# Low parts of 256-column weights placed 192 bytes, not 64, into their buffers

## The chip, the cores and the metric

The kernel runs on one core of a Trainium2 chip. The metric is the device time of one execution in microseconds (us). Before the change it is 1455.13 us, the median of three runs (1454.99 to 1455.19).

## What is computed

A decoder trunk of two layers works on one sequence of 512 tokens with a model width of 1024, all in 32-bit floats. Cut to what matters here:

```
h = rmsnorm(x, g_mix)
z = h @ w_in                      # q, k, v, retention q, k, v, g, two gates
ya = window_attention(...) @ w_a
yb = retention(...) @ w_b
mixed = sigmoid(ga) * ya + sigmoid(gb) * yb
x = x + mixed @ w_out
h2 = rmsnorm(x, g_mlp)
x = x + square(relu(h2 @ w_up)) @ w_down
```

At the end stands one more rmsnorm. Nearly all the arithmetic is in the products with the weight matrices.

## The kernel before, in words

**High and low parts.** TensorE multiplies numbers of a shortened 32-bit type. To keep the precision, every operand is split into a high part (the number rounded to that type) and a low part (the rest, rounded again), and a product of two operands is made of three matmuls: high x high, high x low, low x high. The function `products` (lines 389 to 397) issues the three; line 395 multiplies the first operand's high part with the second's high part, line 396 the first's high part with the second's low part, line 397 the first's low part with the second's high part. In a matmul the first operand is the weights, loaded into TensorE's array by an instruction of its own (PEld in the profile), and the second operand is moved through it column by column. So lines 395 and 396 load the same high part of the weights, and line 397 loads the low part. In the profile's rows the moving operand is named first: `mm<-xl,hi` moves xl past the weights hi.

**Weight units.** The weight matrices come in units of 128 x 1024 numbers. The order of the units is written out in `unit_order`. `load_until` issues their transfers into the buffers `raw`, a few units ahead (AHEAD = 4), and `split_until` (from line 322) makes the parts: ScalarE writes `hi` (line 343), VectorE subtracts and writes `lo` (line 344). `hi` and `lo` have four buffers each (SPLIT + 1). `unit` hands the two parts to the stage that multiplies with them.

**Seven products instead of eight.** The up projection, the down projection, the values of the retention and the output projection (w_out) are made with a block scheme that replaces eight products of half-size blocks by seven products of sums of blocks. The sums of weight blocks are made partly by transfers that add (GpSimd's queue), partly on VectorE. Two of these stages have moving operands of 256 columns, with the weight parts `hi` and `lo` as the weights: the units named "pair" (w_up; the function `pair`, through `products`, lines 395 to 397) and the units named "wo" (w_out; the function `output`, line 1301, which issues hi, hi, lo for each place). In all other stages 512 columns are moved, or `hi` and `lo` are the moving operand.

**Where the parts lie.** A line here is LINE = 16 numbers, 64 bytes in each of the 128 partitions. Each buffer of `hi` and `lo` has UNIT + 4 * LINE = 1088 numbers, 4352 bytes, so that the part can be placed some lines into it:

```
LINE = 16
ASIDE = ("pair", "wo")
...
            aside = LINE if name in ASIDE else 0
            hi, lo = (
                wpool.tile([P, UNIT + 4 * LINE], F32R, tag=n, name=n, bufs=SPLIT + 1)[:, aside : aside + UNIT]
                for n in ("hi", "lo")
            )
```

In the units "pair" and "wo" both parts begin 64 bytes into their buffers, in all others at the buffer's start. In the memory that the program is given, the buffers of `hi` and `lo` and those of the moving operands (`xh`, `xl`, `r0` to `r7`, `late`) all begin 128 bytes past a multiple of 256, and each matmul's columns begin a multiple of 512 bytes further on. So the weights of a matmul lie 64 bytes from its moving rows, modulo 256, in "pair" and "wo", and 0 bytes from them in the rest. This distance is what the text calls the distance.

**The order of the work.** The order on each engine is set when the program is built. In a "pair" stage each of 28 pairs makes 7 x 12 = 84 matmuls of 256 columns (2352), and between two pairs' groups stand the 512-column matmuls of the down projection. "wo" has 7 x 48 = 336 matmuls in each layer (672).

Of the kernel before, what the change touches and what calls it, by code (L numbers as in the profile page):

```python
# [11 lines left out]
F32R = mybir.dt.float32r  # L12
# [5 lines left out]
P = 128  # L18
# [27 lines left out]
N_PAIR = 14  # L46
UNIT = 1024
LINE = 16
ASIDE = ("pair", "wo")
WARM = 8  # L50
PACE = 0.8
DEEP = 3
# [2 lines left out]
SPLIT = 3  # L55
# [62 lines left out]
def decoder(ctx, tc, xT, x_first, w_in, w_rv, w_a, w_b, w_wo, w_up, w_pair, w_down, w_end, tables, decay, band, g_last, out):  # L118
# [4 lines left out]
    wpool = ctx.enter_context(tc.tile_pool(name="wpool", bufs=3))  # L123
# [6 lines left out]
    def f32(ap):  # L130
        return ap.bitcast(F32)
# [36 lines left out]
    def halves(i):  # L168

        return (slice(0, UNIT // 2), slice(UNIT // 2, UNIT)) if i < 3 else (slice(0, UNIT),)  # L170
# [11 lines left out]
    def load_until(n):  # L182
        while state["loaded"] < min(n, len(order)):
            i = state["loaded"]
            layer, name, j = order[i][:3]
            if name == "pair":
                load_part(i)
            elif name == "block":
                load_block(i)
            elif name in MIXING:  # L190
                load_values(i)
            else:
                raws[i] = raw_tile()
                for at in halves(i):
                    queue = nc.scalar if i == 0 and at.start == 0 else nc.sync
                    source = w_end[j] if name == "w_end" else weights[name][layer, j]
                    queue.dma_start(raws[i][:, at], source[:, at])
                    if i < 3:
                        load_x()
            state["loaded"] += 1  # L200
# [77 lines left out]
    def add_part(i):  # L278
        if order[i][3] in (1, 2):
            last = raws.pop(i - 1)  # L280
            at = LEFT if order[i][3] == 1 else RIGHT
            nc.vector.tensor_tensor(raws[i][:, at], last[:, LEFT], last[:, RIGHT], ALU.add)
# [18 lines left out]
    def add_block(i):  # L301
        e, part = order[i][2:]
        if part in (2, 4) and e < N_BLOCK - 1:
            raws[i] = raws.pop(i - 2)
            nc.vector.tensor_tensor(raws[i], raws[i], raws.pop(i - 1), ALU.add)
# [10 lines left out]
    def add_values(i):  # L316
        part = order[i][2]
        if part in (2, 4):
            raws[i] = raws.pop(i - 2)
            nc.vector.tensor_tensor(raws[i], raws[i], raws.pop(i - 4), ALU.add)  # L320

    def split_until(n):
        while state["split"] < min(n, len(order)):
            i = state["split"]
            name, part = order[i][1], order[i][-1]
            if name in MIXING:
                add_values(i)
            load_until(i + AHEAD)
            if name == "pair":
                add_part(i)  # L330
            elif name == "block":
                add_block(i)
            raw = raws[i]
            aside = LINE if name in ASIDE else 0
            hi, lo = (
                wpool.tile([P, UNIT + 4 * LINE], F32R, tag=n, name=n, bufs=SPLIT + 1)[:, aside : aside + UNIT]
                for n in ("hi", "lo")
            )
            for at in (LEFT,) if name == "pair" and part == 3 else halves(i):
                if i == 0 and at.start == 0:  # L340
                    nc.vector.tensor_copy(hi[:, at], raw[:, at])
                else:
                    state["high"] = nc.scalar.activation(hi[:, at], raw[:, at], AF.Copy).ins  # L343
                nc.vector.tensor_tensor(lo[:, at], raw[:, at], f32(hi[:, at]), ALU.subtract)  # L344
            kept = {
                "pair": part < 2,
                "block": name == "block" and part < 4 and order[i][2] < N_BLOCK - 1,
                **{n: name == n and order[i][2] < 4 for n in MIXING},
            }
            if not kept.get(name):  # L350
                raws.pop(i)
            parts[i] = (hi, lo)
            state["split"] += 1

    def unit(name, layer):
        i = state["next"]
        assert order[i][:2] == (layer, name), (order[i], layer, name)
        state["next"] += 1
        hold = state["hold"]
        split_until(i + SPLIT + 1 if hold is None else max(i + 1, min(hold, i + SPLIT + 1)))  # L360
        return parts.pop(i)
# [257 lines left out]
    def layer_body(layer):  # L619
# [1006 lines left out]
        class Ending:  # L1626
# [74 lines left out]
            def first_weights(self):  # L1701
                with tc.issue_after(self.turned):
                    split_until(state["next"] + 1)
# [67 lines left out]

    scaled_input(0, 0)
    split_until(1)
    for u in (2, 3):
        for k in (2 * u - 3, 2 * u - 2):
# [170 lines left out]
```

## Time and profile before

| | |
|---|---|
| median of three runs | 1455.13 us |
| the profiled execution, its own time | 1457.31 us |
| its span, first to last instruction | 1455.2 us |
| mean granted clock of TensorE | 0.999 |
| instructions in the span | 22150 |
| busiest part of the chain that ended last | TensorE (matmuls of the product lines) |

The profile is of one execution. Its page gives the busy time of each engine (PE is TensorE's matmuls, PEld its weight loads, DVE VectorE, ACT ScalarE, POOL GpSimd, SP the engine that issues most transfers), the chain of work that ended last, and the costliest groups of instructions. A row of a group has the line, the engine, the operation, the tiles written and read, the shape, the count, the busy time in us, the mean length of one in ns, and the idle time of the engine before it with what ended that. Matmuls overlap in their pipeline: the length of one in a row is not its share of the time. How fast they follow each other is read from the starts, in the timeline (start in us, length in us, engine, line, tiles, shape, count) or in the chain of waits, where neighbours of one line are merged (start, length, line, count).

### The profile page before, as it was taken

The numbers are of one execution on the slowest core, as the hardware profiler recorded it, in microseconds if no ns is written. First come the engines' busy times: TensorE is split into PE (matmuls) and PEld (weight loads), VectorE is DVE, ScalarE is ACT, GpSimd is POOL, SyncE is SP. The second block draws the span as 40 slices with busy tenths as digits, with TensorE's granted clock in tenths as the row PEclk, the third lists the DMA queues.
The fourth block names the chain that finished last, engine by engine and source line by source line (L and its number), as shares of the span: only waits on it lengthen the run. The fifth ranks groups of instructions, "written<-read, shape, count | busy, mean of one in ns | idle before, by whom it ended". The sixth has DMA issues, their size and how long they took to land.

```text
span 1455.2 us, 22150 instructions
## 1 busy us (share of the span) xinstructions
PE 1443.0 (99%) x8041; PEld 1258.8 (87%) x8041; DVE 1167.0 (80%) x1762; ACT 969.2 (67%) x1592; POOL 222.6 (15%) x329
## 2 busy tenths in 40 slices
PE   9999999999999999999999999999999999999998
PEld 7888888888988999999888888888889799999997
DVE  6978876866998888888778788687778988787885
ACT  6657555543687777777756575565437877777775
POOL 0011012112101111112201110112120011111120
PEclk9999999999999999999999999999999999999999
DMA  7598359799745677666955983797875477777664
GB/s 258 177 290 225 105 165 303 237 247 248 232 124 196 191 200 186 175 182 179 310 177 170 295 222 108 215 293 223 221 214 175 138 202 199 195 193 197 177 188 149
DMA packets 96428, 297.57 MB, mean 204 GB/s; under 512 B 11328, under 2 KB 11456, under 8 KB 90432
## 3 DMA queue, kind: packets, MB, share of 16 engines
q0 software_dynamic: 35936, 125.58, 37.2%
q1 hardware_dynamic: 59664, 169.27, 33.5%
q8 instruction: 63, 1.03, 0.3%
q10 hardware_dynamic: 720, 1.31, 0.2%
q14 instruction: 45, 0.37, 0.1%
HBM read 256.54 MB, written 115.87 MB: 256 GB/s over the span
## 4 chain that ended last, share of the span: by engine, by line
PE 94%; DMA 2%; ACT 2%; DVE 1%; issue 1%; SPq 0%; DVEq 0%; ACTq 0%
PE mm L395 23%; PE mm L396 23%; PE mm L397 22%; PE wo L1301 5%; PE b L395 2%; PE b L396 2%; PE b L397 2%; PE rv L396 2%; PE rv L395 2%; PE rv L397 2%; PE mm L410 2%; DMA raw<-w_pair_in 1%; PE score L778 1%; PE pT L743 1%; PE r L397 1%; PE r L396 1%
## 5 line engine op out<-in xcount | busy, mean ns | idle before, releaser
L343 ACT ACTIVATE hi<-raw 128x1024 fp32r<-128x1024 f32 (+1 forms) x387 | 394.3, 1021 | 257.5 <-PE mm L396 137.1
L344 DVE TENSOR_TENSOR lo<-raw,hi 128x1024 fp32r<-128x1024 f32 (+1 forms) x388 | 452.3, 1173 | 105.8 <-ACT hi L343 104.4
L395 PE MATMUL mm<-xh,hi 128*128 128x512 f32 (+1 forms) x976 | 343.1, 355 | 1.6 <-ACT xh L418 0.9
L396 PE MATMUL mm<-xl,hi 128*128 128x512 f32 (+1 forms) x976 | 343.6, 355 | 0.0
L397 PE MATMUL mm<-xh,lo 128*128 128x512 f32 (+1 forms) x976 | 339.5, 354 | 0.0
L395 PEld LDWEIGHTS mm<-xh,hi 128*128 128x128 f32 x976 | 183.9, 189 | 27.6 <-ACT xh L418 1.6
L396 PEld LDWEIGHTS mm<-xl,hi 128*128 128x128 f32 x976 | 185.0, 190 | 24.2
L397 PEld LDWEIGHTS mm<-xh,lo 128*128 128x128 f32 x976 | 182.7, 188 | 23.6
L397 PE MATMUL mm<-r,lo 128*128 128x256 f32 (+1 forms) x608 | 187.9, 309 | 0.0
L396 PE MATMUL mm<-r,hi 128*128 128x256 f32 (+1 forms) x608 | 187.9, 309 | 0.0
L395 PE MATMUL mm<-r,hi 128*128 128x256 f32 (+1 forms) x608 | 185.6, 309 | 0.5 <-ACT mm L1476 0.5
L395 PEld LDWEIGHTS mm<-r,hi 128*128 128x128 f32 x608 | 114.7, 189 | 8.5 <-ACT mm L1476 0.7
L396 PEld LDWEIGHTS mm<-r,hi 128*128 128x128 f32 x608 | 115.2, 189 | 7.8
L397 PEld LDWEIGHTS mm<-r,lo 128*128 128x128 f32 x608 | 114.1, 188 | 6.2
L1624 POOL DMA_DIRECT2D y<-eu x56 | 62.3, 1351 | 370.8 <-DVE eu L1609 370.2
L396 PE MATMUL mm<-lo,r 128*128 128x512 f32 (+1 forms) x276 | 104.6, 388 | 0.0
L397 PE MATMUL mm<-hi,r 128*128 128x512 f32 (+1 forms) x276 | 101.3, 387 | 0.0
L395 PE MATMUL mm<-hi,r 128*128 128x512 f32 (+1 forms) x276 | 98.4, 390 | 0.9 <-ACT eu L1619 0.6
L395 PE MATMUL b<-hi,r 128*128 128x512 f32 x180 | 70.5, 392 | 1.6 <-DVE eu L1609 1.2
L396 PE MATMUL b<-lo,r 128*128 128x512 f32 x180 | 70.3, 390 | 0.0
L1301 PE MATMUL wo<-r,hi 128*128 128x256 f32 x384 | 68.0, 281 | 0.0
L397 PE MATMUL b<-hi,r 128*128 128x512 f32 x180 | 67.9, 390 | 0.0
(323 smaller groups left out, 2679.5 us busy)
## 6 DMA issues: line engine op xcount, KB each, us to landing
raw<-w_in_in SPq DMA_DIRECT2D x73, 512.0 KB, 5.9
sums_down<-w_down_in POOLq DMA_DIRECT2D x30, 1024.0 KB, 11.6
sums_up<-w_pair_in POOLq DMA_DIRECT2D x56, 512.0 KB, 10.5
raw<-w_down_in SPq DMA_DIRECT2D x45, 512.0 KB, 7.8
raw<-w_pair_in SPq DMA_DIRECT2D x84, 256.0 KB, 3.7
y<-y POOLq DMA_DIRECT2D x63, 256.0 KB, 9.2
y<-eu POOLq DMA_DIRECT2D x61, 256.0 KB, 8.0
raw<-sums_down SPq DMA_DIRECT2D x30, 512.0 KB, 7.3
```

What stands on the lines that cost most here:

```text
L343: state["high"] = nc.scalar.activation(hi[:, at], raw[:, at], AF.Copy).ins
L344: nc.vector.tensor_tensor(lo[:, at], raw[:, at], f32(hi[:, at]), ALU.subtract)
L395: nc.tensor.matmul(ps, ah, bh, start=start and i == 0, stop=False, **more)
L396: nc.tensor.matmul(ps, ah, bl, start=False, stop=False, **more)
L397: latest[0] = nc.tensor.matmul(ps, al, bh, start=False, stop=stop and i == n - 1, **more).ins
L410: latest[0] = nc.tensor.matmul(ps, w[:, cols(j, c)], moving[k][low], start=first, stop=bool(final)).ins
L743: nc.tensor.transpose(pt[:, i * P : (i + 1) * P], sm[:, at : at + P], ident)
L778: nc.tensor.matmul(ps[:, g * w : (g + 1) * w], q_s[g][:, c, at], part[:, keys], start=i == 0, stop=i == 1)
L1301: latest[0] = nc.tensor.matmul(o, w[:, cols], v, start=start and first and n % 2 == 0 and w is hi and v is vh, stop=final and w is lo, ski ...
L1624: nc.gpsimd.dma_start(y[:, 2 * j + m, i * T : (i + 1) * T], t, **how)
```

## The change

In the units "pair" and "wo" the low part begins 3 * LINE = 48 numbers, 192 bytes, into its buffer. The high part stays at 64 bytes. All other units stay at 0. No buffer moves and no size changes; the instructions that carry another address are the 140 subtractions of line 344 that write these low parts and the 1008 matmuls that have them as weights.

```diff
-ASIDE = ("pair", "wo")
+NARROW = ("pair", "wo")
+ASIDE = (LINE, 3 * LINE)
...
             raw = raws[i]
-            aside = LINE if name in ASIDE else 0
             hi, lo = (
-                wpool.tile([P, UNIT + 4 * LINE], F32R, tag=n, name=n, bufs=SPLIT + 1)[:, aside : aside + UNIT]
-                for n in ("hi", "lo")
+                wpool.tile([P, UNIT + 4 * LINE], F32R, tag=n, name=n, bufs=SPLIT + 1)[:, at : at + UNIT]
+                for n, at in zip(("hi", "lo"), ASIDE if name in NARROW else (0, 0))
             )
```

The distance between the low part and the moving rows becomes 192 bytes modulo 256 in these units, that of the high part stays 64.

## The prediction

> **What bounds the kernel now.** I read the page first: which engine is busy, and what the chain that ended last is made of.
>
> ```profile
> PE 1443.0 (99%) x8041; PEld 1258.8 (87%) x8041; DVE 1167.0 (80%) x1762; ACT 969.2 (67%) x1592; POOL 222.6 (15%) x329
> PE 94%; DMA 2%; ACT 2%; DVE 1%; issue 1%; SPq 0%; DVEq 0%; ACTq 0%
> ```
>
> Of the span of 1455.2 us TensorE is idle for 12.2 us, and 94% of the chain is its own work. So the time is the sum of the steps from one matmul's start to the next one's start. What a change does to a step, it does to the end. The change touches matmuls of 256 moving columns only, so the next view is the groups of TensorE by line and shape.
>
> ```profile
> L395 PE MATMUL mm<-r,hi 128*128 128x256 f32 x448 | 125.8, 281 | 0.5 <-ACT mm L1476 0.5
> L397 PE MATMUL mm<-r,lo 128*128 128x256 f32 x448 | 125.7, 280 | 0.0
> L395 PE MATMUL mm<-xh,hi 128*128 128x256 f32 x336 | 94.1, 282 | 0.1
> L397 PE MATMUL mm<-xh,lo 128*128 128x256 f32 x336 | 92.1, 281 | 0.0
> L1301 PE MATMUL wo<-r,hi 128*128 128x256 f32 x384 | 68.0, 281 | 0.0
> L1301 PE MATMUL wo<-r,lo 128*128 128x256 f32 x192 | 53.7, 281 | 0.0
> L1301 PE MATMUL wo<-late,hi 128*128 128x256 f32 x64 | 11.6, 281 | 0.2 <-ACT xh L418 0.2
> L1301 PE MATMUL wo<-late,lo 128*128 128x256 f32 x32 | 8.9, 279 | 0.0
> ```
>
> Lines 395 and 396 hold the same weights, so line 396 has the counts of line 395. That makes 3 x (448 + 336) = 2352 matmuls in the "pair" units and 672 in the "wo" units, 3024 in all. A third of them, 448 + 336 + 192 + 32 = 1008, use a low part as weights. The 281 ns in these rows is the time from a matmul's start to its end; matmuls overlap, so this number says nothing of the step. The step is read from the starts. In the chain of waits the "wo" matmuls stand merged (start, length, count):
>
> ```profile
> 365.69 32.13 PE wo L1301 x273
> 399.78 5.70 PE wo L1301 x48
> ...
> 1086.05 33.92 PE wo L1301 x288
> 1120.85 5.46 PE wo L1301 x48
> ```
>
> 33.92 / 288 = 117.8 ns and 32.13 / 273 = 117.7 ns a step, but 5.46 / 48 = 113.8 ns in the last product of layer 1, with the same shape and the same placement of the weights. (The 48 of layer 0 begin with a wait, so their mean is higher.) The timeline shows the same two speeds in the "pair" units (the rows between are left out, with their count below):
>
> ```profile
> 466.15 0.63 PE L395 MATMUL mm<-hi,r 128*128 128x512 f32 x2
> ...
> 466.74 0.28 PE L396 MATMUL mm<-r,hi 128*128 128x256 f32 x1
> ...
> 467.87 0.28 PE L397 MATMUL mm<-r,lo 128*128 128x256 f32 x1
> ```
> ```profile
> 612.10 0.28 PE L395 MATMUL mm<-r,hi 128*128 128x256 f32 x1
> ...
> 615.98 0.28 PE L396 MATMUL mm<-r,hi 128*128 128x256 f32 x1
> ```
>
> Ten steps from 466.74 to 467.87 make 113 ns each; 33 steps from 612.10 to 615.98 make 117.6 ns. The quick run came after two 512-column matmuls that stood in the midst of 256-column ones. Counted over all starts of the timeline, 246 of the 3024 steps are quick (113 or 114 ns), 2760 take 115 to 119 ns, and 18 hold a wait or the way out of one.
>
> A third speed stands at the kernel's end, where 256 columns of a low or high part are the moving rows and both operands begin at the same place modulo 256 bytes:
>
> ```profile
> 1446.00 0.28 PE L396 MATMUL mm<-lo,r 128*128 128x256 f32 x1
> ...
> 1448.64 0.28 PE L397 MATMUL mm<-hi,r 128*128 128x256 f32 x1
> ```
>
> 22 steps in 2.64 us are 120.0 ns. So the same matmul costs 113, 117.7 or 120 ns, and the last two differ in how the weights lie against the moving rows: 64 bytes apart modulo 256 in "pair" and "wo", 0 apart here.
>
> Why a step can depend on that: the weights for the next matmul are loaded while this one runs, and a load takes as long as 256 columns. The loads behind one-column matmuls show it:
>
> ```profile
> 424.94 0.19 PEld L397 LDWEIGHTS mm<-xh,lo 128*128 128x128 f32 x1
> 425.05 0.19 PEld L395 LDWEIGHTS mm<-xh,hi 128*128 128x128 f32 x1
> ```
>
> The second of these loads can start 0.11 us after the first, about the quick step. With 512 columns the load has twice its time, and I expect nothing of placement there. With 256 columns any delay of either read shows.
>
> **The change part by part.** It moves no instruction. On every engine the rows, their order, their waits and all buffers are the same; 1008 weight loads read, and 140 VectorE instructions write, 128 bytes further in. The distance of the low part from the moving rows goes from 64 to 192 modulo 256; that of the high part stays 64.
>
> The writes first.
>
> ```profile
> L344 DVE TENSOR_TENSOR lo<-raw,hi x388: 677/1217/1229, 6.4 to 1431.6; 128x1024 fp32r<-128x1024 f32 x179, 128x512 fp32r<-128x512 f32 x15
>   PEld mm L396: 0.8, 3
> ```
>
> The 388 subtractions at line 344 hold both placements of before, 0 and 64 bytes in, and median and longest lie 12 ns apart; weight loads waited for them 0.8 us in the whole run. I take nothing for the writes; if each of the 140 cost 12 ns more it would be 1.7 us, on VectorE, which is 80% busy, so it would stay hidden behind TensorE.
>
> The weight loads are the term. 1008 steps load a low part. Of the 2760 middle steps, 920 do. No row shows a distance of 192. The nearest rows bound it: 113.4 ns below (between the 113 and 113.8 of the quick runs: neither read is delayed), and 120.0 ns above (distance 0). So the low loads are worth between 920 x (117.7 - 113.4) = -4.0 us and 920 x (120.0 - 117.7) = +2.1 us. Beside them lies the question of what the high loads do, which themselves don't move: quick and middle runs exist at the same distance, so a run keeps the speed at which it began. If undelayed low loads let whole runs become quick, 2760 x 4.3 = -11.9 us. If low loads end the quick runs, 246 x 4.3 = +1.1 us.
>
> I take the lower bound for the low loads alone, -4.0 us. The reason is thin and I say so: going from distance 0 to 64 took 2.3 ns off a step, so the cost falls as the distance grows, and 192 is further on. The high loads stay at 117.7 since nothing about them moves.
>
> A rule of the Trainium skill speaks against any effect: "SBUF — State Buffer", section "Who interferes with whom", gives TensorE two independent read ports, one for the moving operand and one for weight loads, and says that it never waits on anyone. The rows of 113, 117.7 and 120 ns for one shape don't sit well with it, though none of them alone proves a collision; by that rule the sum would be 0.
>
> Some of a gain is given back where TensorE follows a transfer. The chain of waits passes through these in layer 1:
>
> ```profile
> 1168.77 6.64 DMA raw<-sums_up
> ...
> 1177.38 7.17 DMA raw<-w_pair_in
> ...
> 1325.22 7.22 DMA raw<-w_pair_in
> 1333.86 8.69 DMA raw<-w_down_in
> ```
>
> They cover 29.7 us, 2% of the 94% of the span that the chain spends on TensorE. A quicker TensorE gains nothing there, so I take 2% of a gain back: 0.1 us of 4.0.
>
> The sum: 1455.1 (median) - 4.0 + 0.1 = 1451.2 us. The profiled execution took 1457.31 us beside its span of 1455.2; it lies 2.2 us over the median of 1455.13, and as every term is a difference of steps, I apply the sum to the median.
>
> **The rivals.** First, nothing changes: 1455.1. That holds if the pattern by which the two reads meet repeats every 128 bytes, so that 64 and 192 are the same distance. For it: the four high buffers stand 4352 = 17 x 256 bytes apart, so the 288 even steps from 1086.05 on mix even and odd multiples of 256 bytes, and a shift by 256 costs nothing; the period is 256 or a part of it. 128 is such a part. Against it: nothing in this trace. By the rule of the Trainium skill on the ports, above, this is the case too.
>
> Second, slower. The low loads meet the moving rows as badly as at distance 0: 120.0 ns, +2.1 us, and as a run can stay quick only if none of its loads is delayed, the 246 quick steps fall back to the middle speed, +1.1 us: 1455.1 + 3.2 = 1458.3. It decides from a step of 119.7 ns at the low loads on (1.8 us of 2.9). If the high loads are dragged along, all steps go to 120.0: 2760 x 2.3 + 246 x 6.6 = +8.0 us, 1463.1. For it: high and low parts now lie differently, so the pattern changes twice in every three loads, and the delay of one load shifts the next. Against it: the one known step away from distance 0 helped.
>
> Third, all runs become quick: 1455.1 - 11.9 + 0.2 (the same 2% given back) = 1443.4. For it: 48 quick steps in a row at 1120.85, with high loads at the distance that they keep. Against it: those runs began out of the ordinary order, and two loads of three don't move.
>
> **How the numbers follow.** Low loads undelayed, 1451.2, own range 1449.5 to 1453: 0.31. Nothing changes, 1455.1: 0.29. Slower, 1458 to 1463: 0.28. All quick, 1443.4: 0.12. A measurement of this kernel can tell about 0.2%, 2.9 us, from no change. Faster by more: 0.31 + 0.12 = 0.43; within: 0.29; slower: 0.28. The range reaches from just under the all-quick case, 1443.0, to the middle of the slower case, 1460.5; what is left out is some of the slower case's upper end and little below.
>
> **What would show it.** In the chain of waits of the changed kernel the 288 "wo" steps from about 1086 on: 33.92 us if nothing changes, 33.92 - 96 x 0.0043 = 33.5 with undelayed low loads, 32.7 if all are quick, 34.1 or more if low loads are worse. In the timeline the step in which a low part is loaded (the second of each three) would stand at 113 instead of 118 ns. The 512-column steps and the subtractions at line 344 should keep their times. The forecast is wrong if that second step is not the one that moved, or if the high loads' steps move with it.

## The result and the profile after

The changed kernel takes 1446.14 us (median of four runs, 1445.81 to 1447.65); the kernel before took 1455.16 us beside it (four runs, 1454.99 to 1455.38). The ratio is 0.994, with a 95% interval of 0.9923 to 0.9957: 9.0 us faster. The forecast was 1451.2 us. Sign and range held, and the gain is 2.3 times the forecast one.

The page of the changed kernel first: the busy times, and the engines of the chain that ended last.

```profile
PE 1431.3 (99%) x8041; PEld 1246.5 (86%) x8041; DVE 1166.0 (81%) x1762; ACT 969.6 (67%) x1592; POOL 222.0 (15%) x329
PE 97%; ACT 2%; DVE 1%; DMA 0%; issue 0%; ACTq 0%; DVEq 0%
```

TensorE is 11.7 us less busy (1443.0 before) with the same 8041 instructions, VectorE's 1166.0 us are those of before (1167.0), and the median of the 388 subtractions of line 344 is 1218 ns, 1217 before, so the shifted writes cost nothing that shows. The chain now passes through none of the four transfers of layer 1 that the prediction listed: TensorE has 97% of it, 94% before. The profiled execution took 1446.45 us beside its span of 1444.4, so the span fell by 10.8 us. That execution of before lay 2.2 us above its median, this one 0.3 us above its own; so the two profiles differ by more than the medians.

The "wo" matmuls in the chain of waits of the changed kernel (start, length, count):

```profile
364.28 32.00 PE wo L1301 x282
397.13 5.73 PE wo L1301 x48
...
1079.64 32.67 PE wo L1301 x288
1113.18 5.50 PE wo L1301 x48
```

The 288 steps take 32.67 us, 113.4 ns each; before they took 33.92 us, 117.8 ns. That is the value which the prediction wrote down for the rival in which all runs become quick. The high loads' steps must have moved too, since the low loads' third alone would have stopped at 33.5 us. The timeline shows it in the "pair" units (rows left out between the first three and the last; 40 steps from first to last):

```profile
606.73 0.28 PE L395 MATMUL mm<-r,hi 128*128 128x256 f32 x1
606.84 0.28 PE L396 MATMUL mm<-r,hi 128*128 128x256 f32 x1
606.96 0.28 PE L397 MATMUL mm<-r,lo 128*128 128x256 f32 x1
...
611.26 0.28 PE L397 MATMUL mm<-r,lo 128*128 128x256 f32 x1
```

4.53 us in 40 steps are 113.3 ns; the stretch of before with the same shapes had 117.6. The first three rows show no step in three that stands out: all three are quick. Counted over all starts, 2749 of the 3024 steps are quick now (113 or 114 ns), 246 before; the mean of the steps that hold no wait went from 117.42 to 113.77 ns. In the "wo" units the step in which one high part is loaded while the other's matmul runs went from 117.0 to 113.2 ns, that in which the low part is loaded from 117.6 to 113.3, and the one after it from 117.0 to 114.0.

What is left at the head of a run of 256 columns can be read there as well. A row with x2 holds two matmuls, so from one row to the row after the next there are three steps:

```profile
1079.47 0.40 PE L1301 MATMUL wo<-r,hi 128*128 128x256 f32 x2
1079.71 0.28 PE L1301 MATMUL wo<-r,lo 128*128 128x256 f32 x1
1079.83 0.39 PE L1301 MATMUL wo<-r,hi 128*128 128x256 f32 x2
1080.06 0.28 PE L1301 MATMUL wo<-r,lo 128*128 128x256 f32 x1
1080.17 0.39 PE L1301 MATMUL wo<-r,hi 128*128 128x256 f32 x2
```

The first three steps take 0.36 us, 120 ns each; the next three 0.34 us. After four or five steps the run is quick and stays so to its end. Before, most runs began and ended at 117 to 119 ns. The heads, with all other steps above 113.4 ns that hold no wait, cost about 1.1 us together (342.1 us of steps against 3007 x 113.4 ns).

### The profile page after: what moved, and what is told of

Its sections match the earlier page's. It is cut to its first block, busy times and chain, and to the rows that moved or that the text cites. A ratio compares the mean times of both kernels' runs of the same rounds, so it can differ in the third digit from the quotient of the medians.

```text
span 1444.4 us, 22150 instructions
## 1 busy us (share of the span) xinstructions
PE 1431.3 (99%) x8041; PEld 1246.5 (86%) x8041; DVE 1166.0 (81%) x1762; ACT 969.6 (67%) x1592; POOL 222.0 (15%) x329
## 4 chain that ended last, share of the span: by engine, by line
PE 97%; ACT 2%; DVE 1%; DMA 0%; issue 0%; ACTq 0%; DVEq 0%
PE mm L395 23%; PE mm L396 23%; PE mm L397 23%; PE wo L1301 5%; PE b L395 3%; PE b L396 3%; PE b L397 3%; PE rv L395 2%; PE rv L397 2%; PE rv L396 2%; PE mm L410 2%; PE score L778 1%; PE pT L743 1%; PE r L396 1%; PE r L397 1%; PE r L395 1%
## 5 line engine op out<-in xcount | busy, mean ns | idle before, releaser
L283 DVE TENSOR_TENSOR raw<-raw 128x512 f32<-128x512 f32 x56 | 38.5, 687 | 36.6 <-DMA raw<-w_pair_in 27.8
```

## The experiments

Two theories stood at the start. **Theory 1**: what counts is that successive loads lie unalike; a pattern of delayed steps holds only while each load repeats the last one's place, and a load that lies otherwise throws the run into the quick pattern. **Theory 2**: distance 192 is free of the delay and 64 is not. Theory 2 had a difficulty from the start: the high loads, still at 64, became quick too. In the expectations "hi" and "lo" are the high and low parts, and "slow pattern" is the one of 115 to 120 ns steps.

In every edit below the first number of ASIDE is the high part's place, the second the low part's; the changed kernel has (LINE, 3 * LINE), 64 and 192 bytes. No run leaves out any part of the computation. The numbers are medians, ratios to the kernel before with their 95% intervals, and the mean of the 256-column steps without a wait, worked out from all starts of the one timeline that each run has. The kernel before took 1455.1 to 1455.8 us beside these runs.

**Both parts at 192.**

```diff
-ASIDE = (LINE, 3 * LINE)
+ASIDE = (3 * LINE, 3 * LINE)
```

> High and low parts of "pair" and "wo" both at 192 bytes. Theory 1 (what counts is that successive loads lie unalike: an odd load breaks a slow pattern that holds only while every load lies alike): the loads are alike again, the slow pattern holds, steps of 115 to 120 ns, 1452 to 1463 us, slower than the changed kernel by 6 us or more. Theory 2 (the distance of 192 is free of the delay and that of 64 is not): all loads are at the free distance, steps of 113.3 to 113.8 ns, 1444 to 1447 us, as the changed kernel or a little better.

1455.49 us, 1.0002 (0.9993 to 1.0011), mean step 117.57 ns. Its chain has the very length of before:

```profile
1084.12 33.92 PE wo L1301 x288
```

So 192 alone is no better than 64 alone. Theory 2 falls; the gain needs both places in one kernel.

**The two places exchanged.**

```diff
-ASIDE = (LINE, 3 * LINE)
+ASIDE = (3 * LINE, LINE)
```

> High parts at 192 bytes, low parts at 64: the two places of the changed kernel exchanged. Theory 1 (unlike successive loads): as the changed kernel, steps of 113 to 114 ns, 1445 to 1448 us. Theory 2 (192 is free, 64 is not): two loads of three at the free distance instead of one of three; the changed kernel gained 9.0 us with one, so not more than 1446 us and, if each load counts for itself, below it. If it is the low part's write by VectorE that has to lie apart, it is back at 1455 us.

1446.38 us, 0.9938 (0.9926 to 0.9951), mean step 114.07 ns, and 2573 quick steps. So the gain does not hang on which part lies where. One difference from the changed kernel, which has 2749 quick steps, shows: behind some waits, and once behind 512-column matmuls, a run fell into the pattern of mostly 117 to 119 ns and kept it for 46 to 70 steps. There are five such runs, four of which kept it to their end or their next wait; the changed kernel has none of even 14 steps. One is the last product of "wo" in layer 1:

```profile
1114.96 5.71 PE wo L1301 x48
```

5.71 / 48 = 119.0 ns a step, where the changed kernel needed 5.50 us for the same 48 (above).

**Both at the buffers' start.**

```diff
-ASIDE = (LINE, 3 * LINE)
+ASIDE = (0, 0)
```

> Both parts at their buffers' start, as in all other units: distance 0. By both theories the 120.0 ns step that the 22 matmuls at the kernel's end show holds for all 3024 steps: against the 117.4 ns mean of the kernel before 2.6 ns by 3000 = +7.8 us, about 1463 us. If the 120.0 ns belongs to the kernel's end and not to the distance: 1455 us.

1461.54 us, 1.0042 (1.0029 to 1.0054), mean step 119.79 ns. The 288 steps:

```profile
1087.40 34.56 PE wo L1301 x288
```

34.56 / 288 = 120.0 ns, the price that the prediction read from 22 matmuls at the kernel's end. That price belongs to distance 0.

**High at 0, low at 128.**

```diff
-ASIDE = (LINE, 3 * LINE)
+ASIDE = (0, 2 * LINE)
```

> High parts at distance 0, low parts at 128: the same difference of 128 bytes between high and low as in the changed kernel, with other distances from the moving rows. Theory 1 (unlike successive loads): quick steps of 113 to 114 ns, 1445 to 1448 us. Theory 2 (the distance from the moving rows decides for each load): two loads of three are at the worst distance, steps of 119 to 120 ns with at best one of three quicker, 1456 to 1463 us.

1461.29 us, 1.0034 (1.0021 to 1.0047), mean step 119.13 ns.

```profile
1088.60 34.30 PE wo L1301 x288
```

High and low differ by 128 bytes as in the changed kernel, and nothing is won. Theory 1 in its plain form, that any unlike load will do, falls. The distance and the unlikeness both count.

**The same distances at other places in the memory.** All moving rows but those of "late" go 64 bytes further, and the weights of all units with them.

```diff
-ASIDE = (LINE, 3 * LINE)
+ASIDE = (2 * LINE, 4 * LINE)
...
+    const.tile([P, LINE], F32, name="ahead")
     xh = const.tile([P, KD, T], F32R, name="xh")
...
+    const.tile([P, 3 * LINE], F32, name="behind")
...
-                for n, at in zip(("hi", "lo"), ASIDE if name in NARROW else (0, 0))
+                for n, at in zip(("hi", "lo"), ASIDE if name in NARROW else (LINE, LINE))
```

> The moving rows all lie 64 bytes further on (but for "late"), the weights of every unit too: in "pair" and "wo" hi at 128 and lo at 256 bytes of their buffers. The distances are those of the changed kernel (64 and 192), the places in the memory those of the run with hi at 0 and lo at 128, which took 1461.29 us. If the distance to the moving rows decides: 1445 to 1448 us, and only the 96 steps in "wo" whose moving rows are "late" (distances 128 and 0) are at 118 to 120 ns. If the place in the memory decides: 1459 to 1462 us.

1448.47 us, 0.9947 (0.9935 to 0.9960), mean step 113.93 ns, against 1461.29 us for the run with 0 and 128, whose weights lie at the same two places modulo 256 (high and low exchanged) with the moving rows unshifted. So the distance between weights and moving rows decides, and not the place in the memory. The kernel holds its own control: the moving rows "late" stayed where they were, so their matmuls have distances 128 and 0. The timeline goes through them in the second layer (the line is 1303 here, since the edit adds two lines):

```profile
1106.83 0.39 PE L1303 MATMUL wo<-r,hi 128*128 128x256 f32 x2
...
1107.85 0.40 PE L1303 MATMUL wo<-late,hi 128*128 128x256 f32 x2
1108.09 0.28 PE L1303 MATMUL wo<-late,lo 128*128 128x256 f32 x1
...
1110.57 0.28 PE L1303 MATMUL wo<-late,lo 128*128 128x256 f32 x1
1110.68 0.39 PE L1303 MATMUL wo<-r,hi 128*128 128x256 f32 x2
```

The nine steps ahead of "late" take 1.02 us, 113.3 ns each; the 24 steps of "late" take 2.83 us, 117.9 ns, out of the same weight buffers. Over the kernel the "wo" steps with "late" average 118.4 ns and the others 113.6.

**Alike in each unit, unlike from unit to unit.**

```diff
-                for n, at in zip(("hi", "lo"), ASIDE if name in NARROW else (0, 0))
+                for n, at in zip(("hi", "lo"), (ASIDE[i % 2],) * 2 if name in NARROW else (0, 0))
```

> In each "pair" and "wo" unit high and low parts lie alike, at 64 bytes in the units of even number and at 192 in those of odd number: the loads differ from unit to unit, not within the groups of three. If one load that lies unlike the last breaks the slow pattern and the quick one then keeps itself up: quick from the first change of unit in a run on, most steps at 113.3 to 113.8 ns, 1446 to 1450 us. If each group of three needs its unlike load: the steps are those of the kernel before, 117 to 118 ns, 1454 to 1456 us.

1448.08 us, 0.9948 (0.9936 to 0.9961), mean step 114.82 ns, 1999 quick steps. In each group of three all loads lie alike here, as before, and still two thirds of the steps are quick. The timeline shows where a run turns. The first unit of "wo" is at 64, the second (from 366.43) at 192, the third (from 369.25) at 64:

```profile
365.72 0.40 PE L1301 MATMUL wo<-r,hi 128*128 128x256 f32 x2
...
366.43 0.40 PE L1301 MATMUL wo<-r,hi 128*128 128x256 f32 x2
...
369.25 0.39 PE L1301 MATMUL wo<-r,hi 128*128 128x256 f32 x2
...
370.27 0.39 PE L1301 MATMUL wo<-r,hi 128*128 128x256 f32 x2
```

The six steps from 365.72 to 366.43 are 118 ns each, the 24 from 366.43 to 369.25 are 117.5, the nine from 369.25 to 370.27 are 113.3; the run then stays quick to its first wait. So the change from 64 to 192 left the pattern as it was, and the change back from 192 to 64 turned it. Counted over the kernel (changes with at least six matmuls of one unit, and no wait, on either side), a change from 192 to 64 turned the middle pattern, that of 117 to 119 ns, into the quick one in 17 of 18 cases, a change from 64 to 192 in none of 10; out of the quick pattern, all 72 changes of either direction left it quick. The turn takes some five steps.

**High at 64, low at 128.**

```diff
-ASIDE = (LINE, 3 * LINE)
+ASIDE = (LINE, 2 * LINE)
```

> High parts at 64, low parts at 128 bytes: successive loads differ by 64 bytes instead of 128, and the low load lies at a distance that alone is the worst (120.0 ns with both parts at 0). If any difference between successive loads is enough: 1445 to 1448 us. If the difference has to be 128 and both distances off 0 and 128: two loads of three at 117.4 ns and one at 120.0, mean 118.3 ns, 3000 steps by 0.9 ns over the kernel before: 1457 to 1459 us.

1457.85 us, 1.0016 (1.0007 to 1.0025), mean step 118.42 ns. The sum is that of the second case, and the difference of 64 opens nothing. But the steps are not the two at 117.4 and one at 120.0 of which it was made: the step into the second high part averages 119.2 ns, that into the low part 119.3, and that behind the low part 116.8. Both parts at 128 were not run, so what distance 128 costs alone is not shown; beside two loads at distance 0 (the run with 0 and 128) a load at 128 would come to 117.8 ns, beside two at 64 to 120.4, if each load had a price of its own.

**Two distances between.** Both parts at 32 bytes, and both at 96.

```diff
-ASIDE = (LINE, 3 * LINE)
+ASIDE = (LINE // 2, LINE // 2)
```

> High and low parts of "pair" and "wo" both 32 bytes into their buffers, alike: distance 32. So far, with both parts alike, distance 0 gave steps of 120.0 ns and distances 64 and 192 steps of 117.4 to 117.6 ns. If the price falls evenly from 0 to 64: 118 to 119 ns, 1457 to 1460 us. If the distance has to be a certain time ahead of the moving rows and 32 is that: the quick state at once, 113.3 ns, about 1444 to 1446 us.

1458.75 us, 1.0026 (1.0017 to 1.0035), mean step 118.32 ns, and one quick step in the whole kernel.

```diff
-ASIDE = (LINE, 3 * LINE)
+ASIDE = (3 * LINE // 2, 3 * LINE // 2)
```

> Both parts 96 bytes into their buffers, alike: distance 96, which is 32 bytes short of 128, the other place with the price of 0. If only the nearness to a multiple of 128 counts: as at 32 bytes, 1457 to 1460 us. If the side counts, one of the two at 32 and 96 is quicker than 117.4 ns a step and the other slower.

1454.74 us, 0.9995 (0.9986 to 1.0004), mean step 117.47 ns. Neither case came out whole: 96 costs what 64 costs and 32 costs more, so nearness to a multiple of 128 alone does not decide, and yet neither place is quicker than 64. At no distance tried do alike loads make most runs quick.

**High at 96, low at 224.**

```diff
-ASIDE = (LINE, 3 * LINE)
+ASIDE = (3 * LINE // 2, 7 * LINE // 2)
```

> High parts at 96, low parts at 224 bytes: unlike by 128 bytes as in the changed kernel, around the distance 96, which with both parts alike gave 117.5 ns a step and 1454.74 us. If a difference of 128 opens the quick state wherever the distances alone don't give the 120.0 ns of distance 0: 1444 to 1448 us. If it does so only with 64 and 192: 117 to 119 ns, 1453 to 1459 us, as the pair of 0 and 128 did.

1457.71 us, 1.0012 (1.0003 to 1.0022), mean step 117.88 ns, 66 quick steps. A difference of 128 doesn't open the quick pattern from 96, where alike loads cost the same as at 64. Of the pairs tried only 64 and 192 do.

**The places of the changed kernel in all units.**

```diff
-                for n, at in zip(("hi", "lo"), ASIDE if name in NARROW else (0, 0))
+                for n, at in zip(("hi", "lo"), ASIDE)
```

> High parts at 64 and low parts at 192 bytes in all units, those of the 512-column products too, whose steady step is 226.67 ns, the same rate per column as the quick 256-column step with its fixed part. If the unlike places do for 512 columns what they do for 256: the slower steps at the head of each run of 512 columns (three to seven steps of 228 to 237 ns, some 40 ns a run over some 100 runs) get shorter, 1442 to 1446 us. If the 512-column steps bear no other distance than 0: 4255 of them by up to 4 ns, 1450 to 1463 us.

1462.10 us, 1.0046 (1.0033 to 1.0058). The 256-column steps keep their gain (114.15 ns), but the 512-column steps go from a mean of 227.7 to 231.5 ns: about 4190 steps without a wait by 3.8 ns = 16 us lost.

**64 for both parts in the other units.**

```diff
-                for n, at in zip(("hi", "lo"), ASIDE if name in NARROW else (0, 0))
+                for n, at in zip(("hi", "lo"), ASIDE if name in NARROW else (LINE, LINE))
```

> "pair" and "wo" as in the changed kernel; all other units have both parts at 64 bytes instead of 0, alike, so that their 512-column products have the distance 64 (hi and lo as weights) or 192 (hi and lo as moving rows). If the worst place for 512 columns is the one that is worst for 256 (distance 0): the slower steps at the head of each 512-column run shrink, by up to 4 us in all, 1442 to 1446 us. If alike loads at another distance hold the 512-column steps above 226.67 ns as they hold the 256-column steps at 117.4: the same 3.6 to 4.1 ns by some 4200 steps, 1455 to 1463 us.

1465.04 us, 1.0058 (1.0045 to 1.0072); 512-column steps 231.9 ns, 256-column steps 114.24. Where `hi` and `lo` are the weights (distance 64), the 512-column steps average 233.3 ns; where they are the moving rows (distance 192), 229.7. A long 512-column run with them as the weights in the chain of waits, and then the same run in the changed kernel:

```profile
745.97 8.63 PE mm L410 x37
```
```profile
735.24 8.39 PE mm L410 x37
```

8.63 / 37 = 233.2 ns against 8.39 / 37 = 226.8 ns. At distance 0 a run of 512 columns has a few dear steps at its head and then settles; at 64 it stays dear to its end. The distance that is dearest for 256 columns, of those tried with both parts alike, is the one that works for 512. No kernel of these beats the changed one.

## Why the prediction was right in sign and short in size

**The bound was right.** TensorE's steps set the end: the steps that hold no wait fell by 11 us in the trace (117.42 - 113.77 = 3.65 ns by 3007), and the span by 10.8.

**The low loads' term had the right size by luck.** Their steps did become quick, as the -4.0 us had them. The reason given was that 192 is a better distance than 64, and that is not so: with both parts at 192 the mean step is 117.57 ns, that of before. So the sign came out right without the mechanism. That the range held says little, as from 1443.0 to 1460.5 us it took in three of the four cases whole and a part of the fourth; the favoured case's own range, 1449.5 to 1453 us, was missed by 3.4 us. The 0.1 us given back for transfers does not show: the chain now holds none of the four.

**The step that failed** is "the high loads stay at 117.7 since nothing about them moves", with the sum that took the low loads alone. Their steps went to 113 ns with the low ones, and the prediction had named just that as what would make it wrong. A step is not the price of one load. Both parts at 192 give 1455.49 us and both at 64, beside them, 1455.77, so a priced load would have to cost the same at either place, and then no mixture of the two could gain. The units that alternate show what holds in its place: a run has two patterns of steps, the loads at 64 and those at 192 can run in either, and a pattern that is entered goes on until something disturbs it. In the changed kernel every third step is a return from 192 to 64, the very change that turned 17 of 18 undisturbed runs, and no run stays long in the dear pattern. That the returns do this is argued, not shown, and they are not enough by themselves: with the two places exchanged every third step is such a return too, and five runs stayed dear for 46 to 70 steps. There one load at 64 follows the return before the next 192, in the changed kernel two; whether that is the reason was not tried.

**The reason behind the low loads' price was wrong too**: "the cost falls as the distance grows". With all loads alike it is 119.8 ns at 0, 118.3 at 32, 117.4 at 64, 117.5 at 96 and 117.6 at 192; it doesn't go on falling, and the pair of 0 and 128 stands at 119.1. Nor did it hold that nothing of placement is to be expected at 512 columns, where the load has twice its time: the change touches none of those matmuls, but the last two runs moved their mean from 227.7 to 231.5 and 231.9 ns.

**The rivals.** All runs quick, at 0.12, is what happened: its 32.7 us for the 288 steps were measured as 32.67. Its 1443.4 us were 2.7 us too low: the heads of the runs take back 1.1 us, and 1.1 us more is held by waits inside 256-column runs (4.85 us after, 3.76 before); the rest I can't assign, since the profiles moved by 10.8 us and the medians by 9.0. Its evidence was in the trace: 48 steps in a row at 113.8 ns with all loads at 64 could not be explained by a price of distance 64. The prediction saw that "a run keeps the speed at which it began", and then priced the loads one by one all the same. No change fell with the ratio, and its premise with the pair of runs: places that cost the same alone are not the same place together. Slower did not happen here, but its price of 120.0 ns was real: it is what distance 0 costs.

By the rule of the Trainium skill that the prediction weighed ("SBUF — State Buffer", section "Who interferes with whom": two independent read ports for TensorE, which never waits) all these placements should take the same time. The runs don't agree: the same 3024 matmuls with the same weights and moving rows average 113.77 to 119.79 ns by placement alone.

**What stays open.** The runs read steps, not ports. Why a return from 192 to 64 turns a run and the way from 64 to 192 doesn't, why such returns leave some runs dear when the two places are exchanged, why 96 and 224 don't do what 64 and 192 do, and what inside the memory or the array makes the two patterns, is not settled. That loads and moving rows meet in the memory fits the dependence on their distance, but it is only argued.

## What to carry to other kernels

When one matmul shape shows two speeds in runs of neighbours at the same placement, don't price single instructions: find what lets a run enter the quick pattern, and value the change by the whole run. Place weights against moving rows on purpose, and try pairs of places, since two that cost the same alone can be quick together. Do it for each width by itself: the placement that freed 256 columns cost 512 columns 16 us.

## What the runs showed of the hardware

- A 256-column matmul of this type with its own weight load has a step of 113.3 ns at best, half of the 226.7 ns of 512 columns at best, and of 120.0 ns at distance 0. Both widths also run in a dearer pattern: 117 to 119 ns with both parts at 64, and mostly 230 to 236 ns for 512 columns at distance 64.
- The patterns keep themselves up: with units that alternate, all 72 undisturbed changes left a quick run quick, while runs with all loads alike at 64 held 117 to 119 ns through 288 steps (33.92 us).
- What was worst for 256 columns (distance 0: 119.79 ns against 117.42 at 64) was best for 512 (a mean of 227.7 ns in the changed kernel, against 233.3 at distance 64 and 229.7 at 192).
- Steps of 32 bytes in the placement matter: with both parts alike, 32 costs 118.3 ns, 64 117.4 and 96 117.5.
